# Mixer B's mask inside its scan, the sample's high and low parts in one set of 64 columns, even halves of 544 and 640 logits, norms spread by three copies, and gate loads let go earlier

## The chip, the core and the metric

The kernel runs on one core of a Trainium2 chip. Its engines are TensorE (PE, with its weight loads PEld), VectorE (DVE), ScalarE (ACT), GpSimd (POOL) and SyncE (SP), which issues nearly all DMAs. The metric is the device time of one execution in microseconds. Before the change it is 1721.83 us, the median of three runs (1721.07 to 1722.91).

## The reference

One layer of a streaming encoder is run for a prompt of 1024 tokens and for a sample of 32 new tokens behind a cache of 512. Weights are shared. Cut to what matters here:

```
z = rmsnorm(x) @ w_in            # q, k, v of mixer A; indexer q, k, w; q, k, v of mixer B; two gates

# mixer A: attention over the top-k keys that an indexer scores
score = (relu(q_i . k_i) * w_i).sum(heads);  idx = top_k(score)
o_a   = softmax(q . k[idx] / 8) @ v[idx]

# mixer B: stick-breaking attention, strictly causal
causal = kpos < qpos
sp   = where(causal, softplus(q . k / 8), 0)
tail = reverse_cumsum(sp) - sp
a    = where(causal, exp(log_sigmoid(q . k / 8) - tail), 0)
o_b  = a @ v

h = x + w_out(sigmoid(g_a) * (o_a @ w_ba) + sigmoid(g_b) * (o_b @ w_bb))
y = h + w_down(relu(w_up(rmsnorm(h)))**2)
```

Both mixers have eight heads of 64, the model's width is 1024 and the hidden width 4096. The keys, values and indexer keys are outputs as well.

## The kernel before, in words

**Precision.** Each fp32 operand is held as two parts of TensorE's round fp32 type, a high part (`xh`, `wh`) and the rest (`xl`, `wl`). A product is three matmuls: high by high, high by low, low by high. Casts on ACT make the high parts; subtractions on GpSimd or VectorE make the low ones.

**Stages.** The tokens are nine tiles of rows: eight of 128 for the prompt and one of 32 for the sample (`NEW`, tile 8). `run` (L535) goes through them so:

- the indexer's projections (`index_projection`, L789), with tokens stationary and weights moving, 328 or 256 columns. For the sample's tile, 32 token columns are stationary.
- `spread_rs` (L747): the reciprocal norms of the rows are needed along the free dimension as well. Each of nine tiles of 128 columns is made on GpSimd as `ones` times the norm, and transposed on TensorE.
- projections of mixer B (`project_b`), the indexer's scores (`index_scores`, L852) and a search for the top-k threshold on VectorE and ACT, which runs at low rank beside what follows.
- projections of mixer A (`project_a`, L1065): again tokens stationary, 256 columns, in four passes; `rope_tables` (L997) makes four tables of rotary factors before.
- mixer B: for each head `attend` (L1176) takes query tiles `t` of 128, with L = 128(t + 1) keys. The logits are made in pieces of 512 columns (PSUM banks `s`). `attend_new` (L1240) does the sample for four heads at once, over 512 cached and 32 new keys (`LS` = 544).
- mixer A: the same, in two passes over the heads, with softmax and the bfloat16 masks of the top-k.
- merge of the branches, the output projection, and the feed-forward part.

**Mixer B's weights** (`stick_weights`, L1146). ACT makes p = sigmoid(z) and rem = sigmoid(-z) from the logits. The reverse products of `rem` are a scan on VectorE, and GpSimd multiplies `p` with `rem` moved by one. The mask is added to the logits in PSUM before that, by one more matmul: `identr` stationary, and the triangle `trir` of -1e30 moving, 128 columns, on the tile's last piece (`tri4r`, 32 columns, for the sample). Then p is 0 and rem is 1 where a key isn't causal:

```
nc.vector.tensor_tensor_scan(rv, rv, rv, 1.0, op0=ALU.mult, op1=ALU.bypass)
nc.gpsimd.tensor_mul(p[:, 0:L - 1], p[:, 0:L - 1], rem[:, 1:L])
```

**What sets the order.** The program is not issued as it is written. Class `Plan` records every instruction as a node with its dependencies and a rank (FAST, PREP, MAIN, FILL, SLOW). It then issues each engine's nodes in order of a guessed time, by its own table of durations: the node that is ready first and, among the ready ones, the one of the lowest rank. Each engine then works through its list in that order. Work that can stand anywhere is used as filling for TensorE. `gate` (L1302) makes one of 16 blocks of 128 gate channels, whose matmuls write `pj` at rank FILL; ACT then takes a sigmoid, except for gates kept raw. Four are made before mixer B, four at its start, six beside its heads (`GATES_BESIDE`), and the last two, with 24 branch products, beside mixer A's heads (`FILL_BESIDE`). A DMA recorded inside `behind` or `held` is planned no earlier than a given node; `behind` takes the last node recorded, so a gate written after head h loads its weights no earlier than that head's end in the plan. Weights go through three buffers `wst`, ACT's cast into `wh` and a subtraction into `wl`, of which there are five pairs.

Every instruction goes through one line of `issue`, so nearly all rows of the profile carry L431; groups are told apart by the names of their tiles.

Of the kernel before, what the change touches and what calls it, by code (L numbers as in the profile page):

```python
# [13 lines left out]
I32 = mybir.dt.int32  # L14
AF = mybir.ActivationFunctionType
# [35 lines left out]
B11, B21, T1, T2, T3, T4, B22 = range(7)  # L51
FAST, PREP, MAIN, FILL, SLOW = 0, 1, 2, 3, 4


def rows(s):

    return DEC if s == NEW else 128

# [40 lines left out]
class Plan:  # L99
# [60 lines left out]
    def tile(self, pool, shape, dtype, name, tag=None, bufs=1, fine=False):  # L160
        tag = tag or name
        kw = {} if pool[2] is None and pool[3].startswith("d") else {"tag": tag, "bufs": bufs}
        t = pool[0].tile(shape, dtype, name=name, **kw)
        words = 1
        for s in shape[1:]:
            words *= s
        if dtype == BF16:
            words = (words + 1) // 2
        if kw:
            ring = self.rings.setdefault((pool[3], tag), [])  # L170
            old = ring[-bufs].touched if len(ring) >= bufs else ()
            psum = pool[3].startswith("ps") and not fine
            m = Mem(1 if psum else 4, 1 if psum else words, old, self.floors[pool[2]])
            ring.append(m)
        else:
            m = Mem(1, words * shape[0])
        self.mem[t.tensor.name] = m
        if pool[3].startswith("ps"):
            self.banks.add(t.tensor.name)
        if kw:  # L180
            self.onchip.add(t.tensor.name)
        self.members[pool[3]].append(m)
        return t


    def cells(self, ap):
        m = self.mem.get(ap.tensor.name)
        if m is None:
            return None
        if m.writer.shape == (1, 1):  # L190
            return m, slice(0, 1), slice(0, 1)
        size = 2 if ap.dtype == BF16 else 4
# [18 lines left out]
        return m, part, np.unique(idx) if size == 2 else idx  # L211
# [239 lines left out]
class Layer:  # L451
# [74 lines left out]

    def x_of(self, k, cs):
# [7 lines left out]
    def run(self):  # L535
# [24 lines left out]
        self.tri4r = nc.tile(self.wpool, [128, DEC], F32R, "tri4r")  # L560
# [8 lines left out]
        self.ones = c([128, 128], F32, "ones")  # L569
        nc.vector.memset(self.ones, 1.0)  # L570
        self.ident = c([128, 128], F32, "ident")
        self.identr = c([128, 128], F32R, "identr")
        self.trir = c([128, 128], F32R, "trir")
# [13 lines left out]
        for i, n in enumerate((W1, T - W1)):  # L587
            self.xh.append(nc.tile(xp, [128, KB, n], F32R, f"xh{i}"))
# [50 lines left out]
        self.att = self.pr = nc.open("att", "right")  # L639
        for _ in range(GATES_FIRST):  # L640
            self.gate(next(gates), "gz", 3)
        for h in range(H):
# [3 lines left out]
            with nc.behind():  # L646
# [22 lines left out]

        for h in range(H):  # L670
# [18 lines left out]
        self.ft = nc.tile(rp, [128, FWORDS], F32, "ft")  # L689
        self.turn = cycle(["pj", "a", "b", "c"])  # L690
# [11 lines left out]
    def constants(self):  # L702
        nc, a = self.nc, self.a
        for name, dst, n in (("tri", self.trir, 128), ("tri4", self.tri4r, DEC)):
            st = nc.tile(self.wpool, [128, 512], F32, name, tag="wst", bufs=3)
            nc.sync.dma_start(st[:, :n], a[name])
            nc.scalar.copy(dst, st[:, :n])
        nc.scalar.copy(self.identr, self.ident)
        nc.sync.dma_start(self.gf, a["g_ffn"])

    def normalise(self, sl):
# [4 lines left out]
        for hf in range(2):  # L716
# [7 lines left out]
            for kk in range(4):  # L724
# [22 lines left out]
    def spread_rs(self):  # L747

        nc = self.nc
        for sl in GROUPS:  # L750
            pt = self.bank("t")
            n = sum(rows(s) for s in sl)
            for i, s in enumerate(sl):
                b = nc.tile(self.ip, [128, 5 * HD], F32, "rsb", tag="ta", bufs=2)[:, :128]
                nc.gpsimd.tensor_scalar(b, self.ones, self.rs[:, s:s + 1], None, op0=ALU.mult)
                m = rows(s)
                nc.tensor.transpose(pt[:, i * 128:i * 128 + m], b[:m], self.ident[:m, :m])
# [3 lines left out]
    def index_setup(self):  # L761
# [9 lines left out]
        self.iw = [[None] * KB, None]  # L771

# [16 lines left out]
    def index_projection(self, part, s):  # L789
# [4 lines left out]
        if self.iw[part] is None:  # L794
# [7 lines left out]
            nc.scalar.copy(self.kih[:, T:], kc)  # L802
            nc.vector.tensor_sub(self.kil[:, T:], kc, self.kih.bitcast(F32)[:, T:])
# [4 lines left out]
        for k in range(KB):  # L808
            xh, xl = self.x_of(k, ts_)
            wh, wl = ws[k]  # L810
            nc.tensor.matmul(ps[:m, :n], xh, wh[:, :n], start=k == 0, stop=False)
            nc.tensor.matmul(ps[:m, :n], xh, wl[:, :n], start=False, stop=False)
            nc.tensor.matmul(ps[:m, :n], xl, wh[:, :n], start=False, stop=k == KB - 1)
# [21 lines left out]
        if part == 0:  # L835
# [6 lines left out]
            nc.scalar.copy(self.kih[:, ts_], pk[:, :m])  # L842
            nc.vector.tensor_sub(self.kil[:, ts_], pk[:, :m], self.kih.bitcast(F32)[:, ts_])

    def key_chunks(self, t):

        if t < 8:
            L = 128 * (t + 1)
            return [(c, min(512, L - c), c) for c in range(0, L, 512)]
        return [(0, PAST, T), (PAST, DEC, SEQ)]  # L850
# [99 lines left out]
    def top_k(self):  # L950

        nc, tp, tx, size = self.nc, self.top, self.top, self.size
        minus = nc.tile(tp, [128, 1], F32, "minus")
        nc.vector.memset(minus, -1.0)
        for g in self.groups:
# [19 lines left out]
            for j, t in enumerate(g.tiles):  # L975
# [13 lines left out]
                nc.scalar.activation(sq[:m, :L], pre[:m, :L], AF.Relu, bias=self.ones[:m, 0:1], scale=-1.0)  # L989
# [7 lines left out]
    def rope_tables(self):  # L997
# [9 lines left out]
        for j in range(2):  # L1007
            nc.vector.tensor_mul(self.tc_[:, :, j], C, g[:, j].unsqueeze(1).to_broadcast([128, NT, HD]))
            gx = g[:, j].rearrange("p (s e) -> p s e", s=2)[:, ::-1, :].unsqueeze(1).to_broadcast([128, NT, 2, 32])
            nc.vector.tensor_mul(  # L1010
# [54 lines left out]
    def project_a(self, p):  # L1065
# [7 lines left out]
        for s in range(NT):  # L1073
            m = rows(s)
            ts_ = slice(128 * s, 128 * s + m)
            ps = self.bank(PA_BANKS[s % len(PA_BANKS)])
            for k in range(KB):
                xh, xl = self.x_of(k, ts_)
                wh, wl = (u[:, (k % 2) * 256:(k % 2) * 256 + 256] for u in units[k // 2])
                nc.tensor.matmul(ps[:m, :256], xh, wh, start=k == 0, stop=False)  # L1080
                nc.tensor.matmul(ps[:m, :256], xh, wl, start=False, stop=False)
                nc.tensor.matmul(ps[:m, :256], xl, wh, start=False, stop=k == KB - 1)
# [63 lines left out]
    def stick_weights(self, parts, L, p, rem):  # L1146
# [6 lines left out]
        nc.vector.tensor_tensor_scan(rv, rv, rv, 1.0, op0=ALU.mult, op1=ALU.bypass)  # L1153
# [22 lines left out]
    def attend(self, h, is_a, passes=(0, 1)):  # L1176
# [17 lines left out]
        def weights(t, q, *room):  # L1194
# [3 lines left out]
            for c0 in range(0, L, 512):  # L1198
                n = min(512, L - c0)
                tail = not is_a and c0 + n == L  # L1200
                ps = self.bank("s")
                nc.tensor.matmul(ps[:, :n], qh, kk[:, c0:c0 + n], start=True, stop=False)
                nc.tensor.matmul(ps[:, :n], ql, kk[:, c0:c0 + n], start=False, stop=not tail)
                if tail:
                    nc.tensor.matmul(ps[:, n - 128:n], self.identr, self.trir, start=False, stop=True)
# [3 lines left out]
            return self.stick_weights(parts, L, *room)  # L1209

        for i in passes:
# [25 lines left out]
            with nc.rank(FAST):  # L1237
                nc.sync.dma_start(self.do[g, :, 512 * i:512 * i + 512], o)

    def attend_new(self, u, is_a):  # L1240
# [13 lines left out]
        kn = nc.tile(at, [128, 4, DEC], F32R, "kn", bufs=1)  # L1254
        nc.sync.dma_start(kn.bitcast(F32), self.dk[g0:g0 + 4, :, :, new].rearrange("j s e t -> (s e) j t"))
        for j in range(4):
# [3 lines left out]
            k = nc.tile(at, [128, SEQ], F32R, "kc", tag="k", bufs=3)[:, :PAST]  # L1260
            nc.scalar.copy(k[:HD], k32[:, j % 2])
            nc.gpsimd.tensor_sub(k[HD:], k32[:, j % 2], k.bitcast(F32)[:HD])
# [6 lines left out]
        parts = [(0, ps0[:, :]), (PAST, ps1[:, :DEC])]  # L1269
        if is_a:  # L1270
            p = self.softmax_weights(parts, LS, self.mask[8], self.fqs[:, u:u + 1], *self.rooms(is_a))
        else:
            nc.tensor.matmul(ps1[:, :DEC], self.identr, self.tri4r, start=False, stop=True)
            p = self.stick_weights(parts, LS, *self.rooms(is_a))
# [450 lines left out]
def _host_arrays(inp):  # L1725
# [45 lines left out]
    out["tri4"] = np.where(np.arange(DEC)[None, :] >= (i % DEC)[:, None], np.float32(NEG), np.float32(0)).astype(np.float32)  # L1771
    out["tri"] = np.where(i[None, :] >= i[:, None], np.float32(NEG), np.float32(0)).astype(np.float32)
# [36 lines left out]
```

## Time and profile before

| | |
|---|---|
| Median of three runs | 1721.83 us |
| The profiled execution, alone | 1724.92 us |
| Its span, first to last instruction | 1723.0 us |
| Mean granted TensorE clock | 0.997 |
| Chain that ended last, TensorE's share | 87% |
| Mixer B, first to last mask matmul | 484 to 686 us of the span |
| Table loads on ACT | 16, 20.5 us in all |
| DMA traffic | 289.08 MB, 168 GB/s |

A row of a group reads: line, engine, operation, tiles out<-in, shapes, count, then the busy time of the group, the mean duration of one in ns, and the idle time of the engine before them. A row of a timeline reads: start, duration, engine, line, operation, tiles, shapes, count of merged instructions. TensorE's matmuls overlap: a duration holds the way through the array, so the distance between starts says what one costs in a stream. A row of a table by stage gives, for each engine, busy time and instructions in that stretch, then the granted clock of TensorE, and the share and rate of the DMA engines.

### The profile page before, as it was taken

What the parts mean: (1) busy time and instruction counts of PE and PEld (TensorE: products, weight loads), DVE (VectorE), ACT (ScalarE), POOL (GpSimd) and SP (SyncE); (2) the same over time, 40 slices, a digit from 0 to 9 for tenths busy, and PEclk for the clock granted to TensorE, in tenths of its full rate; (3) what the DMA queues carried; (4) which work ended last, traced back from release to release, by engine and by line L of the source; (5) the groups of instructions that cost most, each with busy time, mean ns of one, the idle gap of its engine ahead of it and who ended that gap; (6) DMA issues with size and microseconds to landing.
All of it is one profiled execution on the core that took longest, in us unless ns stands there. A gap on an engine that the chain in (4) does not pass through costs nothing.

```text
span 1723.0 us, 34981 instructions
## 1 busy us (share of the span) xinstructions
PE 1691.1 (98%) x12356; PEld 1606.2 (93%) x12356; DVE 1346.7 (78%) x2773; ACT 952.8 (55%) x2023; POOL 854.2 (50%) x703
## 2 busy tenths in 40 slices
PE   7999999999999999999999999999999999999998
PEld 7988999899989899988999999999999999989998
DVE  8666899988568778775765648999988888797756
ACT  7455788765357768886655446333333444425431
POOL 5533331344367777365568757533333456556420
PEclk9999999999999999999999999999999999999999
DMA  7234453354673646686874643534443587756744
GB/s 255 82 100 126 128 161 116 89 151 139 172 207 101 172 103 173 177 243 190 243 213 148 179 135 116 165 135 152 136 153 132 189 286 245 266 169 232 255 127 149
DMA packets 182527, 289.08 MB, mean 168 GB/s; under 512 B 30800, under 2 KB 62128, under 8 KB 182352
## 3 DMA queue, kind: packets, MB, share of 16 engines
q1 hardware_dynamic: 182064, 286.50, 54.1%
q8 instruction: 98, 1.61, 0.4%
q14 instruction: 77, 0.63, 0.1%
q10 hardware_dynamic: 288, 0.34, 0.1%
HBM read 193.59 MB, written 93.07 MB: 166 GB/s over the span
## 4 chain that ended last, share of the span: by engine, by line
PE 87%; DVE 6%; DMA 3%; issue 1%; ACT 1%; POOL 1%; SPq 0%; DVEq 0%; ACTq 0%; POOLq 0%
PE pj L431 35%; PE s L431 11%; PE c L431 11%; PE b L431 10%; PE a L431 10%; PE t L431 5%; PE o L431 4%; DMA q<-dq 1%; DMA k<-cka 1%; DVE y L431 1%; DVE junk L431 1%; DVE us L431 1%; DVE mh L431 1%; DVE xl L431 1%; DMA xt<-x 0%
## 5 line engine op out<-in xcount | busy, mean ns | idle before, releaser
L431 POOL TENSOR_TENSOR wl<-wst,wh 128x512 fp32r<-128x512 f32 x160 | 229.5, 1440 | 231.0 <-ACT wh L431 172.3
L431 PE MATMUL pj<-xl,wh 128*128 128x272 f32 (+2 forms) x1200 | 336.4, 314 | 0.0
L431 PE MATMUL pj<-xh,wh 128*128 128x272 f32 (+1 forms) x768 | 253.3, 330 | 0.4 <-ACT sq L431 0.4
L431 PE MATMUL pj<-xh,wl 128*128 128x272 f32 (+1 forms) x768 | 252.6, 329 | 0.0
L431 PEld LDWEIGHTS pj<-xl,wh 128*128 128x128 f32 x1200 | 213.3, 189 | 11.4
L431 ACT CAST wh<-wst 128x512 fp32r<-128x512 f32 x213 | 131.1, 620 | 140.6 <-PE pj L431 23.4
L431 PEld LDWEIGHTS pj<-xh,wh 128*128 128x128 f32 x768 | 145.2, 189 | 11.5 <-ACT sq L431 0.7
L431 PEld LDWEIGHTS pj<-xh,wl 128*128 128x128 f32 x768 | 145.0, 189 | 10.5
L431 POOL TENSOR_TENSOR p<-p,rem 128x383 f32<-128x383 f32 (+8 forms) x66 | 110.7, 1697 | 31.8 <-DVE rem L431 25.1
L431 DVE TENSOR_TENSOR tt<-t,tt 128x512 fp32r<-128x512 f32 (+2 forms) x168 | 100.1, 620 | 33.2 <-ACT tt L431 32.7
L431 POOL TENSOR_TENSOR wl<-y,wh 128x512 fp32r<-128x512 f32 x49 | 72.9, 1490 | 96.1 <-ACT wh L431 93.0
L431 DVE TENSOR_TENSOR_SCAN rem<-rem 128x384 f32<-128x384 f32 (+8 forms) x66 | 110.6, 1696 | 9.7 <-ACT rem L431 9.6
L431 ACT CAST tt<-t 128x512 fp32r<-128x512 f32 (+2 forms) x168 | 85.8, 539 | 40.8 <-PE t L431 37.5
L431 ACT CAST wh<-y 128x512 fp32r<-128x512 f32 x79 | 49.1, 621 | 106.1 <-issue 23.0
L431 ACT CAST wh<-us 128x512 fp32r<-128x512 f32 x64 | 39.7, 622 | 114.6 <-PE pj L431 27.6
L431 PE MATMUL o<-tt,v 128*128 128x256 f32 (+1 forms) x640 | 99.0, 280 | 3.9 <-ACT tt L431 3.5
L431 ACT ACTIVATE junk<-score,cand 128x1024 bf16<-128x1024 f32 (+2 forms) x93 | 96.9, 1042 | 9.7 <-DVE cand L431 8.4
L431 PE MATMUL s<-k,q 128*128 128x512 f32 (+3 forms) x384 | 100.7, 357 | 1.3 <-DMA q<-dq 1.0
L431 PEld LDWEIGHTS o<-tt,v 128*128 128x128 f32 x640 | 91.8, 191 | 9.9 <-ACT tt L431 4.1
L431 DVE TENSOR_SCALAR_CACHE_REDUCE junk<-score,cand 128x384 bf16<-128x384 f32 (+1 forms) x124 | 92.9, 749 | 3.1
L431 PE MATMUL t<-ident,p 128*128 128x128 f32 (+1 forms) x596 | 91.0, 276 | 0.8 <-POOL p L431 0.6
L431 POOL TENSOR_TENSOR wl<-us,wh 128x512 fp32r<-128x512 f32 x33 | 50.3, 1533 | 71.3 <-ACT wh L431 71.3
(359 smaller groups left out, 5666.5 us busy)
## 6 DMA issues: line engine op xcount, KB each, us to landing
us<-w_down SPq DMA_DIRECT2D x80, 256.0 KB, 3.1
q<-dq SPq DMA_DIRECT2D x64, 256.0 KB, 4.9
du<-y SPq DMA_DIRECT2D x56, 264.0 KB, 2.5
du<-us SPq DMA_DIRECT2D x56, 264.0 KB, 2.5
y<-w_up SPq DMA_DIRECT2D x44, 256.0 KB, 2.7
k<-dk SPq DMA_DIRECT2D x40, 256.0 KB, 5.0
v<-dv SPq DMA_DIRECT2D x40, 256.0 KB, 4.4
xl<-du SPq DMA_DIRECT2D x35, 264.0 KB, 5.3
```

Source lines behind the costliest of these rows:

```text
L431: fn(*args, **kw)
```

## The change

1. Mixer B's mask leaves TensorE and moves into the scan: the state becomes max(state * rem, first), where `first` is a byte tensor that is 1 at the diagonal key and 0 elsewhere, and starts at 0. Keys that aren't causal give 0, the diagonal 1, and the products start there. One column of `p` is set to 0 by a memset, since its neighbour has no `rem`.
2. For the sample's tile, high and low parts stand side by side in `xh` as 64 stationary columns, so two matmuls for each block of the weights make four products (low by low too) in 64 rows, in place of three matmuls. `join` adds the lower 32 rows to the upper: an ACT copy and a VectorE add. The indexer's keys of the sample stand behind the cached ones.
3. Rows of 640 logits are made as 320 + 320 and those of 544 as 272 + 272 (`cut`). The sample's new keys get a DMA for each head into the tile of the cached ones.
4. `spread_rs` makes the broadcast norms of a group of tiles by one VectorE copy. The rotary tables' products move from VectorE to GpSimd.
5. A gate beside head h of mixer B is held to the end of that head's first pass rather than its second. The first piece of filling of mixer A is planned before its first head instead of after it.

```
+def cut(L):
+    return L // 2 if L in (640, LS) else 512
+MIDS = 1
+FILL_AHEAD = 1
-FILL_BESIDE = (1,1,1,1,2,2,2,2,2,2,2,2,2,2,2,1)
+FILL_BESIDE = (0,1,1,1,2,2,2,2,2,2,2,2,2,2,2,1)

+    def token_rows(self, ps, s, ws):
+        mm = self.nc.tensor.matmul
+        if s == NEW:
+            for k in range(KB):
+                x = self.xh[1][:, k, SEQ - W1:]
+                for i in range(2):
+                    mm(ps[:2 * DEC], x, ws[k][i], start=k + i == 0, stop=k + i == KB)
+            return
...
+    def join(self, ps, low):
+        self.nc.scalar.copy(low, ps[DEC:2 * DEC])
+        self.nc.vector.tensor_add(ps[:DEC], ps[:DEC], low)
...
+        if sl[-1] == NEW:
+            nc.scalar.copy(self.xh[1][:, :, T - W1:], self.xl[1].bitcast(F32)[:, :, SEQ - W1:])

         for _ in range(GATES_FIRST):
             self.gate(next(gates), "gz", 3)
+        self.mid = [None] * 3
         for h in range(H):
             self.attend(h, False)
             if h in (2, 5):
                 self.attend_new(h // 3, False)
-            with nc.behind():
+            with nc.held(self.mid[MIDS]):
                 for _ in range(GATES_BESIDE[h]):
                     self.gate(next(gates), "gz", 3)
...
+        beside(FILL_AHEAD)
         for h in range(H):
             self.attend(h, True, (0,))
             beside(FILL_BESIDE[h])
...
+            b = nc.tile(self.pr, [128, 2, 512], F32R, "rsb", tag="zz", bufs=2).bitcast(F32)[:, 0]
+            nc.vector.tensor_copy(b, self.rs[:, sl[0]:sl[-1] + 1].unsqueeze(2).to_broadcast([128, len(sl), 128]))
             for i, s in enumerate(sl):
-                nc.gpsimd.tensor_scalar(b, self.ones, self.rs[:, s:s + 1], None, op0=ALU.mult)
...
-            nc.vector.tensor_mul(self.tc_[:, :, j], C, g[:, j].unsqueeze(1).to_broadcast([128, NT, HD]))
+            nc.gpsimd.tensor_mul(self.tc_[:, :, j], C, g[:, j].unsqueeze(1).to_broadcast([128, NT, HD]))
...
-        nc.vector.tensor_tensor_scan(rv, rv, rv, 1.0, op0=ALU.mult, op1=ALU.bypass)
+        nc.vector.tensor_tensor_scan(rv, rv, one, 0.0, op0=ALU.mult, op1=ALU.max)
+        nc.vector.memset(p[:, L - 1:L], 0.0)
         nc.gpsimd.tensor_mul(p[:, 0:L - 1], p[:, 0:L - 1], rem[:, 1:L])
...
-            for c0 in range(0, L, 512):
+            for c0 in range(0, L, cut(L)):
-                if tail:
-                    nc.tensor.matmul(ps[:, n - 128:n], self.identr, self.trir, start=False, stop=True)
...
+            self.mid = self.mid[1:] + [len(nc.nodes) - 1]
...
-        nc.sync.dma_start(kn.bitcast(F32), self.dk[g0:g0 + 4, :, :, new].rearrange("j s e t -> (s e) j t"))
+            nc.sync.dma_start(k.bitcast(F32)[:, PAST:], self.dk[g0 + j, :, :, new].rearrange("s e t -> (s e) t"))
-                nc.tensor.matmul(ps0, q, k, start=first, stop=last)
-                nc.tensor.matmul(ps1[:, :DEC], q, kn[:, j], start=first, stop=is_a and last)
+                nc.tensor.matmul(ps0[:, :LS // 2], q, k[:, :LS // 2], start=first, stop=last)
+                nc.tensor.matmul(ps1[:, :LS // 2], q, k[:, LS // 2:], start=first, stop=last)
```

The plan is made anew, and with it the order on every engine up to the merge; from the merge on each engine's list is as it was. In number TensorE has 114 matmuls fewer, VectorE 73 instructions more, SP 11 DMAs more, and ACT loads its function tables 6 times in place of 16.

ACT, where mixer B ends and mixer A's first softmax begins (`gz` are the gates' sigmoids, `p,nb<-p,nb,fq` the softmax's exponentials, which use another table). Before:

```order
L431 ACTIVATE gz<-gz 128x512
L431 ACT_TABLE_LOAD
L431 ACTIVATE p,nb<-p,nb,fq 128x384
L431 COPY o<-o 64x256
L431 CAST tt<-t 128x512 x2
L431 ACTIVATE p,nb<-p,nb,fq 128x512
L431 ACT_TABLE_LOAD
L431 ACTIVATE gz<-gz 128x272
L431 ACT_TABLE_LOAD
L431 ACTIVATE p,nb<-p,nb,fq 128x128
```

And now:

```order
L440 ACTIVATE gz<-gz 128x272
L440 COPY o<-o 64x256
L440 CAST tt<-t 128x512 x2
L440 ACT_TABLE_LOAD
L440 ACTIVATE p,nb<-p,nb,fq 128x384
L440 COPY o<-o 64x256
L440 CAST tt<-t 128x512
L440 CAST tt<-t 128x384
L440 ACTIVATE p,nb<-p,nb,fq 128x512
```

The last gate sigmoids have moved ahead of the first exponential, so one table load stands there and no other follows until the merge.

SP, in the first pass of mixer A, where the sample's cached keys are loaded (`k_...<-cka`, two heads in each; `kn` and `kc<-dk` are the new keys; `wst<-w_bb` weights of the filling). Before:

```order
L431 DMA wst<-w_bb 128x512
L431 DMA gz<-dg 128x512
L431 DMA kn<-dk 128x4x32
L431 DMA k_7444<-cka 64x2x512
L431 DMA k_7447<-cka 64x2x512
L431 DMA dg<-gz 128x512
L431 DMA wst<-w_bb 128x512
```

And now:

```order
L440 DMA q<-dq 64x2x512
L440 DMA dg<-gz 128x512
L440 DMA k_7395<-cka 64x2x512
L440 DMA wst<-w_bb 128x512
L440 DMA k_7398<-cka 64x2x512
L440 DMA gz<-dg 128x512
L440 DMA dg<-gz 128x512
L440 DMA do<-o 64x512
L440 DMA wst<-w_bb 128x512
```

A load of weights has come between the two loads of cached keys, and new keys are no longer fetched at once beside them.

More of the change, by code (lines that the diff above doesn't have):

```diff
@@ L191, in cells @@
             return m, slice(0, 1), slice(0, 1)
-        size = 2 if ap.dtype == BF16 else 4
+        size = SMALL.get(ap.dtype, 4)
         dims = list(ap.ap)
@@ L210, in cells @@
         idx = idx * size // 4
-        return m, part, np.unique(idx) if size == 2 else idx
+        return m, part, np.unique(idx) if size < 4 else idx
     @staticmethod
@@ L559, in run @@
         self.gf = s([128, KB], "gf")
-        self.tri4r = nc.tile(self.wpool, [128, DEC], F32R, "tri4r")
+        self.eye4 = nc.tile(self.wpool, [128, DEC], F32, "eye4")
         w("wh3", "wl3")
@@ L639, in run @@
         self.att = self.pr = nc.open("att", "right")
+        self.first = nc.tile(self.att, [128, T], U8, "first")
+        nc.gpsimd.memset(self.first[:, DEC:SEQ + DEC - 128], 0)
+        nc.scalar.copy(self.first[:, :DEC], self.eye4)
+        nc.scalar.copy(self.first[:, SEQ + DEC - 128:], self.ident)
         for _ in range(GATES_FIRST):
             self.gate(next(gates), "gz", 3)
+        self.mid = [None] * 3
         for h in range(H):
@@ L689, in run @@
         self.ft = nc.tile(rp, [128, FWORDS], F32, "ft")
+        self.ones = nc.tile(rp, [128, 128], F32, "sum")
+        nc.vector.memset(self.ones, 1.0)
         self.turn = cycle(["pj", "a", "b", "c"])
@@ L703, in constants @@
         nc, a = self.nc, self.a
[L704 to L708, printed above, removed]
+        nc.sync.dma_start(self.eye4, a["eye4"])
         nc.sync.dma_start(self.gf, a["g_ffn"])
@@ L771, in index_setup @@
         self.iw = [[None] * KB, None]
+        self.ones = nc.tile(ik, [128, 128], F32, "ones")
+        nc.vector.memset(self.ones, 1.0)
     def index_weights(self, js):
@@ L807, in index_projection @@
         ps = self.bank("s")
[L808 to L813, printed above, removed]
+        self.token_rows(ps[:, :n], s, [[z[:, :n] for z in w] for w in ws])
+        if s == NEW:
+            self.join(ps[:, :n], nc.tile(self.wpool, [128, 512], F32, "pl", tag="wst", bufs=3)[:DEC, :n])
         w = nh * HD
@@ L952, in top_k @@
         nc, tp, tx, size = self.nc, self.top, self.top, self.size
-        minus = nc.tile(tp, [128, 1], F32, "minus")
+        minus, plus = (nc.tile(tp, [128, 1], F32, z) for z in ("minus", "plus"))
         nc.vector.memset(minus, -1.0)
+        nc.vector.memset(plus, 1.0)
         for g in self.groups:
@@ L1074, in project_a @@
             m = rows(s)
-            ts_ = slice(128 * s, 128 * s + m)
             ps = self.bank(PA_BANKS[s % len(PA_BANKS)])
[L1077 to L1082, printed above, removed]
+            self.token_rows(ps[:, :256], s, [
+                [u[:, i * 256:i * 256 + 256] for u in unit] for unit in units for i in range(2)])
+            if s == NEW:
+                self.join(ps[:, :256], nc.tile(pr, [128, 4, HD], F32, "pl", tag="sq", bufs=1).rearrange("p h e -> p (h e)")[:DEC])
             sq = nc.tile(pr, [128, 4, HD], F32, "sq", bufs=1)
@@ L1144, in softmax_weights, with stick_weights @@
         return p
-    def stick_weights(self, parts, L, p, rem):
+    def stick_weights(self, parts, L, p, rem, one):
         nc, at = self.nc, self.att
@@ L1208, in weights @@
                 return self.softmax_weights(parts, L, self.mask[t], self.fq[:, t, h:h + 1], room[0])
-            return self.stick_weights(parts, L, *room)
+            return self.stick_weights(parts, L, *room, self.first[:, DEC + SEQ - L:][:, ::-1])
         for i in passes:
@@ L1272, in attend_new @@
         else:
-            nc.tensor.matmul(ps1[:, :DEC], self.identr, self.tri4r, start=False, stop=True)
-            p = self.stick_weights(parts, LS, *self.rooms(is_a))
+            p = self.stick_weights(parts, LS, *self.rooms(is_a), self.first[:, :LS])
         pt = self.bank("t")
@@ L1770, in _host_arrays @@
     i = np.arange(128)
-    out["tri4"] = np.where(np.arange(DEC)[None, :] >= (i % DEC)[:, None], np.float32(NEG), np.float32(0)).astype(np.float32)
-    out["tri"] = np.where(i[None, :] >= i[:, None], np.float32(NEG), np.float32(0)).astype(np.float32)
+    out["eye4"] = (DEC - 1 - np.arange(DEC)[None, :] == (i % DEC)[:, None]).astype(np.float32)
     return out
```

56 lines of the change are left out of this document (29 added, 27 removed).

## The prediction

> **What bounds the kernel now.** I read the page's busy shares and the shares of its chain first.
>
> ```profile
> PE 1691.1 (98%) x12356; PEld 1606.2 (93%) x12356; DVE 1346.7 (78%) x2773; ACT 952.8 (55%) x2023; POOL 854.2 (50%) x703
> ...
> PE 87%; DVE 6%; DMA 3%; issue 1%; ACT 1%; POOL 1%; SPq 0%; DVEq 0%; ACTq 0%; POOLq 0%
> ```
>
> TensorE is busy for 98% of the span and carries 87% of the chain that ends last. No other engine comes near: VectorE, the next, has 78%. A matmul taken from TensorE's queue should therefore come off the end, wherever it stands, if nothing else takes its place. Busy time hides small gaps, so the second view is busy time by stage.
>
> ```profile
> core 0: us, PE busy (x) PEld busy (x) DVE busy (x) ACT busy (x) POOL busy (x), PEclk, DMA share, GB/s
> 0.00:90.00 90.00, 80.51 (x552) 74.75 (x553) 63.48 (x191) 51.80 (x134) 48.15 (x62) 1.00 0.50 161
> ...
> 300.00:340.00 40.00, 35.78 (x261) 33.17 (x260) 37.42 (x131) 30.32 (x62) 13.46 (x16) 0.96 0.29 91
> ...
> 485.00:694.00 209.00, 208.12 (x1447) 192.55 (x1447) 175.00 (x201) 154.47 (x364) 162.73 (x102) 1.00 0.54 147
> 694.00:740.00 46.00, 44.89 (x317) 41.46 (x317) 30.91 (x120) 42.81 (x83) 12.40 (x20) 1.00 0.68 190
> 740.00:897.00 157.00, 153.07 (x1048) 140.71 (x1046) 110.04 (x351) 108.36 (x227) 97.80 (x98) 0.99 0.78 223
> ...
> 950.00:1723.00 773.00, 761.31 (x6017) 749.82 (x6015) 626.02 (x996) 312.94 (x639) 367.48 (x265) 1.00 0.55 179
> ```
>
> The stages are the indexer's projections (0 to 90), part of mixer A's projections with the top-k counts (300 to 340), mixer B (485 to 694), the start of mixer A (694 to 740), the rest of it, and the merge with the feed-forward part. TensorE idles 9.5 us in the first (90 - 80.51), 4.2 in the second, 0.9 in mixer B, 1.1 and 3.9 in mixer A and 11.7 after 950. So 773 of the 1723 us hold no edit, and what is edited lies in stages where TensorE waits little.
>
> **The change part by part.** In a stream of matmuls the price of one is the distance from its start to the next start; its mean duration in the groups also holds the pipeline's depth. I take distances from timelines.
>
> *Masks.* 64 matmuls of 128 columns go (the tile `trir`), and two of 32 columns.
>
> ```profile
> 524.63 0.40 PE L431 MATMUL s<-k,q 128*128 128x256 f32 x2
> 524.87 0.22 PE L431 MATMUL s<-trir,identr 128*128 128x128 f32 x1
> 524.93 0.57 PE L431 MATMUL s<-k,q 128*128 128x384 f32 x2
> 525.34 0.28 PE L431 MATMUL o<-tt,v 128*128 128x256 f32 x1
> 525.46 0.22 PE L431 MATMUL s<-trir,identr 128*128 128x128 f32 x1
> 525.51 0.34 PE L431 MATMUL pj<-xh,wh 128*128 128x272 f32 x1
> 525.69 0.29 PE L431 MATMUL pj<-xl,wh 128*128 128x272 f32 x1
> ...
> 525.94 0.29 PE L431 MATMUL pj<-xh,wh 128*128 128x272 f32 x1
> ...
> L431 PE MATMUL s<-trir,identr 128*128 128x128 f32 x64 | 15.4, 240 | 0.0
> ```
>
> The mask at 525.46 is followed after 0.05 us, but the 272-column matmul behind it takes 0.18 instead of the 0.125 of each of the two after it (525.69 to 525.94): the short mask leaves no room to hide the next weight load. A mask thus costs 0.05 + 0.05 = 0.10 us, and by the pair at 524.87 0.06 + 0.06 (0.41 for two of 384 columns, against about 0.35 by the steps below). I take 0.11, so 66 x 0.11 = 7.3 us. Bounds are the bare distance, 66 x 0.05 = 3.3, and the group's whole 15.4.
>
> The Trainium skill, "TensorE: Matmul & The Clock Gate", section Back-to-back issue gap, gives N / 2.4 + 2.5 ns for a single matmul, about 56 ns at 128 columns; by that rule masks would be an estimated 3.7 us and the sum below 15.4. Its section on LDWEIGHTS gives columns / 1.2, which is 107 ns for 128 stationary columns, and the 0.10 to 0.12 measured above sides with it.
>
> *The sample's parts.* In each of six projections 24 matmuls of 32 stationary columns become 16 of 64.
>
> ```profile
> 313.06 0.28 PE L431 MATMUL s<-wh,xh 128*32 128x256 f32 x1
> 313.18 0.28 PE L431 MATMUL s<-wl,xh 128*32 128x256 f32 x1
> ...
> 315.86 0.29 PE L431 MATMUL pj<-xl,wh 128*128 128x272 f32 x1
> ...
> 51.01 0.31 PE L431 MATMUL s<-ih,xh 128*128 128x328 f32 x1
> 51.16 0.32 PE L431 MATMUL s<-il,xh 128*128 128x328 f32 x1
> ...
> L431 ACT COPY o<-o 64x256 f32<-64x256 f32 x68 | 25.1, 369 | 35.2 <-PE o L431 32.4 <-DMA do<-o 1.1 <-PE pj L431 0.6
> ```
>
> The 24 run from 313.06 to 315.86, 2.80 us or 0.117 each; a third less is 0.93, in five projections of 256 columns 4.7. The sixth has 328 columns at 0.15, so 8 x 0.15 = 1.2. Together 5.9 us. No row has 64 stationary columns, but 32 and 128 cost the same per moving column, so I put 64 there: the bounds are 5.9 and, if a matmul of 64 took half as long again, zero. Added is the join: an ACT copy and a VectorE add of 32x256, 0.37 us by the copy's row and about as much for the add, behind each projection. If TensorE had to wait for all six, that is 6 x 0.8 = 4.8 us; I cost it at nothing, because the next projection's `pj` matmuls stand in the queue. One copy of 8x32 columns into `xh` is added as well, once, of the same size.
>
> The skill's "TensorEngine Tiling (Array Packing)", section Key Properties, says that changing the tiling mode drains TensorE, which speaks against odd column counts: with a drain of 0.28 us (the flight time of the row at 313.06) on entering and leaving each of the six groups, an estimated 3.4 us, the sum below would be 15.6. No run here shows 64 columns, but the trace shows no such gap where the 32-column group ends.
>
> *Halves.* 512 + 128 columns become 320 + 320, and 512 + 32 become 272 + 272.
>
> ```profile
> 759.02 0.63 PE L431 MATMUL s<-k,q 128*128 128x512 f32 x2
> 759.49 0.40 PE L431 MATMUL pj<-xh,wh 128*128 128x512 f32 x1
> 759.72 0.34 PE L431 MATMUL s<-k,q 128*128 128x128 f32 x2
> 759.89 0.45 PE L431 MATMUL pj<-xl,wh 128*128 128x512 f32 x1
> 760.18 0.40 PE L431 MATMUL pj<-xh,wl 128*128 128x512 f32 x1
> ...
> 549.32 1.04 PE L431 MATMUL s<-kn,qz 128*128 128x32 f32 x8
> 550.21 0.26 PE L431 MATMUL s<-tri4r,identr 128*128 128x32 f32 x1
> ```
>
> A tile of 640 costs 0.47 for two of 512, 0.17 for two of 128 and 0.06 on the matmul behind them (0.29 instead of 0.23), 0.70 in all. 320 columns lie between 272 at 0.125 and 328 at 0.15, so four cost 4 x 0.147 = 0.59; 16 tiles save 16 x 0.11 = 1.8. For the sample the eight of 32 columns take 0.89 us, 0.11 each, as a full weight load would: a pair is 0.235 + 0.11 against 2 x 0.125, and 32 pairs save 3.1. In the indexer the same two cuts are made in eight heads each; the saving lies between nothing and 8 x 0.11 + 16 x 0.1 = 2.5, and I take 0.9. Halves together: 5.8 us, bounds 4.9 and 7.4.
>
> *VectorE, GpSimd, ACT.*
>
> ```profile
> L431 DVE TENSOR_TENSOR_SCAN rem<-rem 128x1024 f32<-128x1024 f32 x8 | 20.3, 2532 | 3.5 <-ACT rem L431 3.5
> L431 DVE TENSOR_TENSOR_SCAN pre<-sq,minus 128x1024 f32<-128x1024 bf16 x1 | 2.3, 2290 | 0.3 <-ACT sq L431 0.3
> ...
> 485.00:694.00 209.00, 110.58 (x66) 47.61 (x100) 109.92 (x66) 1.00 0.54 147
> ...
> L431 DVE MEMSET ss<- 128x9 f32 x1 | 0.1, 66 | 0.0
> L431 DVE TENSOR_TENSOR tabc<-ropec,gqk 128x576 f32<-128x576 f32 x2 | 1.5, 741 | 0.0
> ...
> L431 POOL TENSOR_TENSOR wl<-wst,wh 128x512 fp32r<-128x512 f32 x160 | 229.5, 1440 | 231.0 <-ACT wh L431 172.3
> ...
> L431 ACT ACT_TABLE_LOAD x11 | 14.1, 1283 | 0.2
> ```
>
> The scan gets a one-byte second operand and a maximum in place of a bypass. The one row with a narrower operand (bf16, 2290 ns) is not slower than the fp32 scans of that length (2532, some of them waiting), so I take no change. Bounds are the same time and, since nothing shows a byte operand, twice it (the last rival). The row of mixer B is that of instructions on `rem` alone, VectorE's first: scans hold it for 110.6 of 209 us. The 66 memsets of one column cost at most 66 x 0.066 = 4.4 us there, in the 34 us that VectorE idles (209 - 175.0). Spreading the norms takes nine products from GpSimd and gives VectorE three copies. The four rotary products (4 x 0.74 us) leave VectorE just before the stretch in which it is busy 37.42 of 40 us, and cost GpSimd about 4 x 1.6 (1440 ns for 512 columns, here 576), where it is busy 13.5 of 40; what they delay there is the low halves of weights, up to 6 us, and those are prepared ahead in five pairs of buffers. I cost both at nothing.
>
> The gates' loads are let go half a head earlier, and the first fill before mixer A's first head. By the order of instructions the last gate sigmoids then stand ahead of the first softmax, and ten of the table loads between 694 and 740 go: 10 x 1.28 = 12.8 us of ACT. ACT is busy 42.81 of those 46 us, but TensorE waits only 1.1, so this is worth 0 to 1.1 us. I count nothing.
>
> The sum is 7.3 + 5.9 + 5.8 = 19.0 us of TensorE. The profiled execution took 1724.92 us with its span of 1723.0, 3.1 over the median of 1721.83. It would come to 1705.9, and the median to 1702.8.
>
> **The rivals.** *Stalls shrink too.* ACT freed, VectorE relieved by 3 us around 300 to 340, fills earlier.
>
> ```profile
> PE t L431 <- DVE vt L431: 2.3, 1, 2.3
> ...
> 795.81 8.93 DMA k<-cka
> ```
>
> In the stretch 300 to 340 TensorE's longest wait, 2.3 us, is for VectorE, and its clock is at 0.96, which is another 0.04 x 40 = 1.6 us. In mixer A the cached keys take 8.93 us to land and ACT waits for them with the casts that TensorE needs behind it. All waits of 300 to 340 and 694 to 897 with the lost clock are 4.2 + 1.6 + 1.1 + 3.9 + 1.6 = 12.4; half of it gone gives 1697. Against it: the queue still issues those keys one weight load ahead of their cast.
>
> The skill's first page named above says in Part 1 that a few microseconds without work halve the clock for a window of about 3.4 us; the 0.96 behind that wait agrees.
>
> *New stalls take part of it.* The scheduler laid out the first 940 us anew, and its idea of times missed by 2 to 4 us at two places. Against 19.6 us of waits there now (9.5 + 4.2 + 0.9 + 1.1 + 3.9), half as many again makes 1713; twice as many would leave the time where it was.
>
> *The work goes, but not from the path*, so that the time stays within 0.2%, about what a measurement of this kernel can tell from none: it needs TensorE waiting about 16 us more, against 98% busy.
>
> *Slower: the scan.* If a one-byte operand or the maximum makes the scan slower, VectorE becomes mixer B's bound. It has 34 us of room less 4 for memsets, so this decides from a scan 27% slower (30 of 110.6), costs back the 19 from 45%, and at twice the time adds 110.6 - 30 = 81, so 1784. The bf16 row speaks against it.
>
> **How the numbers follow.** The forecast (1699 to 1708) has 0.55, shrinking stalls 0.17, new stalls 0.18, no change 0.05 and the slow scan or anything slower 0.05. The predicted time is 1703. The bounds of the costs (masks 3.3 to 15.4, joins up to 4.8) widen it to 1694 to 1713, which leaves out the last two cases and the ends of the others. Faster has 0.9, within 0.2% 0.05, slower 0.05.
>
> **What would show it.** TensorE's count must fall by 114. In mixer B a scan of 1024 should stay at 2.3 to 2.6 us and VectorE under 185. The 64-column matmuls should follow each other at 0.117 us, those of 320 at 0.147. Table loads should be 6, not 16. The rows from 950 on should keep their length; if TensorE's idle time before 950 is over 28 us, the new order made stalls, and if it is under 14, it took some away. The prediction is wrong if the span falls by less than 10 us or more than 28.

## The result, and the profile after

| | before | changed |
|---|---|---|
| median, us | 1721.8 (1721.07 to 1722.91) | 1705.38 (1703.88 to 1707.35) |
| ratio | | 0.9901, 95% interval 0.9889 to 0.9914 |
| profiled execution, us (span) | 1724.92 (1723.0) | 1703.88 (1702.1) |

The change gains 16.4 us by the medians; 1703.0 was forecast, and the forecast's own range of 1699 to 1708 holds the time. The two profiled executions differ by 21.0: that of before lies 3.1 over its median, that of the changed kernel 1.5 under. So 4.6 us of what two traces show is spread between executions.

The page of the changed kernel, busy shares and chain:

```profile
PE 1671.8 (98%) x12242; PEld 1591.3 (93%) x12242; DVE 1349.7 (79%) x2846; ACT 942.4 (55%) x2019; POOL 847.7 (50%) x699
...
PE 85%; DVE 8%; issue 2%; DMA 2%; ACT 1%; POOL 1%; SPq 0%; DVEq 0%; ACTq 0%; POOLq 0%
```

TensorE has the 114 matmuls less that were counted, and 19.3 us less busy time. Its idle time, the span less that, is 30.3 us where it was 31.9 (1723.0 - 1691.1). The same comes from distances between matmul starts. As the time of a matmul I take (columns + 29) / 2.4 ns, a fit to the distances measured (0.125 us at 272 columns, 0.146 at 320), but no less than 0.11 us, the distance at which those of 128 or 32 columns follow each other. What the distances exceed this by, where it is over 60 ns, adds up to 65.9 us of waits before and 63.1 now, stretches at half clock included; the rest of the stream is 17.8 us shorter. The split rests on that fit: without the 0.11 the rest would be 14.5 us shorter.

Busy time by stage of the changed kernel, with bounds where its stages lie now (busy us of each engine, TensorE's clock, DMA share, GB/s):

```profile
0.00:84.00 84.00, 75.39 (x515) 71.01 (x516) 65.95 (x187) 52.33 (x132) 42.08 (x52) 1.00 0.54 172
...
300.00:340.00 40.00, 38.07 (x290) 35.74 (x289) 38.75 (x137) 30.81 (x64) 15.07 (x18) 1.00 0.37 105
...
474.00:690.00 216.00, 214.04 (x1481) 198.47 (x1481) 179.50 (x269) 156.05 (x368) 157.61 (x102) 1.00 0.53 145
690.00:736.00 46.00, 41.73 (x284) 36.49 (x283) 39.42 (x167) 40.97 (x107) 21.43 (x36) 1.00 0.84 230
736.00:882.00 146.00, 144.82 (x1015) 134.50 (x1014) 100.73 (x307) 98.45 (x193) 91.05 (x86) 1.00 0.78 231
...
913.00:1702.00 789.00, 777.53 (x6144) 766.10 (x6143) 641.00 (x1012) 320.21 (x655) 382.08 (x276) 1.00 0.54 178
```

The last stage, 789 us with 11.5 of idle, is what it was. In the 40 us of top-k counts TensorE idles 1.9 us where it idled 4.2, and its clock is back at 1.00. After the start of mixer A it idles 1.2 where it idled 3.9. At that start itself the reverse has come: 4.3 us of 46, against 1.1. Between the same events of the two programs, 3.9 us go up to the top-k counts, 6.8 from there to mixer B's first scan, and 10.2 in the two mixers.

What the prediction named, by group (count, busy us, mean ns of one | idle of the engine before them):

```profile
L440 DVE TENSOR_TENSOR_SCAN rem<-rem,first 128x1024 f32<-128x1024 f32 x8 | 21.9, 2742 | 3.0 <-ACT rem L440 1.8 <-POOL p L440 1.1
L440 DVE MEMSET p<- 128x1 f32 x66 | 3.8, 59 | 6.0 <-ACT p L440 3.3 <-DMA dg<-gz 2.4
L440 POOL TENSOR_TENSOR tabs<-ropes,gqk 128x576 f32<-128x576 f32 x2 | 2.9, 1438 | 0.0
L440 ACT ACT_TABLE_LOAD x6 | 7.7, 1283 | 3.8 <-DMA gz<-dg 2.0 <-PEq L1819 1.7
```

And the sample's columns of one projection, where they begin on TensorE's timeline (start, us, stationary rows * columns):

```profile
312.08 0.28 PE L440 MATMUL s<-wh,xl 128*128 128x256 f32 x1
312.20 0.28 PE L440 MATMUL s<-wh,xh 128*64 128x256 f32 x1
312.31 0.28 PE L440 MATMUL s<-wl,xh 128*64 128x256 f32 x1
```

The scan's mean is above the 2532 of before, and above the 2.3 to 2.6 us that the prediction set as its mark. But the eight differ much among themselves, from 2287 to 3521 ns now and from 2292 to 2984 then, and the shortest are alike. All 66 scans take 113.9 us, where they took 110.6. VectorE is busy 179.5 of mixer B's 216 us. The 64-column matmuls follow each other at 0.11 to 0.12 us.

### The profile page after: what moved, and what is told of

It is laid out like the page before. It is cut to its first block, busy times and chain, and to the rows that moved or that the text cites. A ratio compares the mean times of both kernels' runs of the same rounds, so it can differ in the third digit from the quotient of the medians.

```text
span 1702.1 us, 34820 instructions
## 1 busy us (share of the span) xinstructions
PE 1671.8 (98%) x12242; PEld 1591.3 (93%) x12242; DVE 1349.7 (79%) x2846; ACT 942.4 (55%) x2019; POOL 847.7 (50%) x699
## 4 chain that ended last, share of the span: by engine, by line
PE 85%; DVE 8%; issue 2%; DMA 2%; ACT 1%; POOL 1%; SPq 0%; DVEq 0%; ACTq 0%; POOLq 0%
PE pj L440 35%; PE c L440 11%; PE b L440 10%; PE a L440 10%; PE s L440 10%; PE o L440 5%; PE t L440 5%; DVE junk L440 2%; DVE y L440 1%; DVE mh L440 1%; DVE us L440 1%; POOL wl L440 0%; SPq L440 0%; DVE wl L440 0%; DVE small L440 0%
## 5 line engine op out<-in xcount | busy, mean ns | idle before, releaser
L440 PEld LDWEIGHTS pj<-xh,wh 128*128 128x128 f32 x768 | 144.6, 188 | 10.2 <-DVE gz L440 0.3
L440 POOL TENSOR_TENSOR p<-p,rem 128x383 f32<-128x383 f32 (+8 forms) x66 | 101.8, 1562 | 45.3 <-DVE rem L440 34.3
L440 DVE TENSOR_TENSOR_SCAN rem<-rem,first 128x384 f32<-128x384 f32 (+8 forms) x66 | 113.9, 1748 | 7.5 <-ACT rem L440 6.3
L440 ACT ACTIVATE junk<-score,cand 128x1024 bf16<-128x1024 f32 (+2 forms) x93 | 97.0, 1043 | 12.3 <-DVE cand L440 10.7
L440 PE MATMUL s<-k,q 128*128 128x512 f32 (+4 forms) x384 | 97.9, 353 | 5.6 <-DVE nb L440 3.0
```

What stands on the lines that cost most here:

```text
L440: fn(*args, **kw)
```

## The experiments

The gain of each is against runs of before on the same chip. Busy is TensorE's on the page of the profiled execution, idle the span less that.

| kernel | median, us | gain | ratio (95%) | busy | idle |
|---|---|---|---|---|---|
| changed | 1705.38 | 16.4 | 0.9901 (0.9889 to 0.9914) | 1671.8 | 30.3 |
| changed, again | 1705.89 | 15.5 | 0.9911 (0.9895 to 0.9926) | 1668.7 | 32.5 |
| masks back on TensorE | 1709.99 | 12.4 | 0.9926 (0.9914 to 0.9939) | 1678.0 | 30.5 |
| masks of zeros added | 1712.79 | 9.6 | 0.9942 (0.9930 to 0.9955) | 1677.8 | 33.3 |
| sample in 32 columns | 1709.91 | 12.4 | 0.9922 (0.9907 to 0.9937) | 1673.3 | 28.8 |
| halves cut at 512 | 1710.91 | 11.4 | 0.9930 (0.9918 to 0.9943) | 1676.1 | 30.4 |
| gates as before | 1711.17 | 10.3 | 0.9936 (0.9923 to 0.9949) | 1675.9 | 35.1 |
| norms, rotary as before | 1713.18 | 8.2 | 0.9947 (0.9936 to 0.9959) | 1673.8 | 39.2 |
| before, mask alone | 1722.35 | -0.9 | 1.0004 (0.9996 to 1.0013) | 1685.9 | 34.7 |
| before, mask, order kept | 1717.32 | 4.2 | 0.9975 (0.9963 to 0.9986) | 1686.6 | 30.8 |
| before, side edits alone | 1715.26 | 6.2 | 0.9969 (0.9958 to 0.9981) | 1687.9 | 28.7 |
| changed, side edits undone | 1718.16 | 3.3 | 0.9978 (0.9969 to 0.9988) | 1676.1 | 40.6 |
| changed, filling let go earlier | 1701.99 | 21.0 | 0.9873 (0.9853 to 0.9893) | 1670.9 | 31.6 |

### Each cut in TensorE's stream undone

Masks back:

```
-        nc.vector.tensor_tensor_scan(rv, rv, one, 0.0, op0=ALU.mult, op1=ALU.max)
-        nc.vector.memset(p[:, L - 1:L], 0.0)
+        nc.vector.tensor_tensor_scan(rv, rv, rv, 1.0, op0=ALU.mult, op1=ALU.bypass)
...
+                if tail:
+                    nc.tensor.matmul(ps[:, n - 128:n], self.identr, self.trir, start=False, stop=True)
```

> The changed kernel with mixer B's mask back on TensorE (66 matmuls) and the old scan without the memset of one column. If the masks cost what the prediction says, 0.11 us each in the stream, the time is 1705.4 + 7.3 = 1712.7 us. If only their own distance to the next start counts (5.2 us by the trace of before), 1710.6. If the new scan and its memsets took something of it back on VectorE, less than 1710. If the order made anew matters more than the matmuls, anything within 4 us of 1712.7, with TensorE's waits before 950 us differing from the changed kernel's by that much.

Masks of zeros, which leave the scan of the change in place:

```
+                if tail:
+                    nc.tensor.matmul(ps[:, n - 128:n], kk[:, :128], self.zero.unsqueeze(1).to_broadcast([128, 16, 8]), start=False, stop=True)
```

> The changed kernel, scan and all, with 66 matmuls put where the masks were, which add zeros to the logits (for stationary columns the keys, for moving ones a tile of zeros): the masks' price on TensorE by itself. Theory: 1705.4 + 7.3 = 1712.7 us, as for the kernel with the masks back; own distance alone: 1710.6. If the scan of the change costs VectorE something that the end sees, this kernel is slower than the one with the masks and the old scan, by that.

The sample in 32 columns (`join` and the copy into `xh` go too):

```
-                for i in range(2):
-                    mm(ps[:2 * DEC], x, ws[k][i], start=k + i == 0, stop=k + i == KB)
...
+            xh, xl = self.x_of(k, slice(128 * s, 128 * s + rows(s)))
```

> The changed kernel with the sample's projections as before: 24 matmuls of 32 stationary columns in place of 16 of 64, no join. The product of the two low parts is left out, as before. Theory: 48 matmuls at 0.117 to 0.15 us, 1705.4 + 5.9 = 1711.3 us. Rival, that the joins cost TensorE up to 0.8 us each: 1705.4 + 5.9 - 4.8 = 1706.5.

Halves:

```
-    return L // 2 if L in (640, LS) else 512
+    return 512
...
-                nc.tensor.matmul(ps0[:, :LS // 2], q, k[:, :LS // 2], start=first, stop=last)
+                nc.tensor.matmul(ps0[:, :PAST], q, k[:, :PAST], start=first, stop=last)
```

> The changed kernel with rows of 640 logits as 512 + 128 and of 544 as 512 + 32 again. Theory: 1705.4 + 5.8 = 1711.2 us, of which 3.1 from the sample's logits, 1.8 from the attention's 640 and 0.9 from the indexer. Rival: the short matmuls lay in gaps that are there anyway, 1705 to 1707.

With the changed kernel at 1705.6 (the mean of its two medians) they cost 4.4, 7.2, 4.3 and 5.3 us, each uncertain by some 3 (its own interval and the changed kernel's together). In the traces, waits set aside, the stream grows by 7.4, 6.6, 5.1 and 5.4. The prices of the prediction (7.3, 7.3, 5.9, 5.8) are right to within a microsecond, in the stream. The times by themselves don't settle a mask's price: the kernel with the masks back (1710.0) came out near the bare distance (1710.6), that with masks of zeros (1712.8) at the theory (1712.7). Of the masks undone the end saw 3.0 us less than the stream, no more than the uncertainty. Whether the new scan costs anything at the end isn't settled either: the two kernels with masks differ by 2.8 us, and their intervals overlap. On VectorE the 66 scans take 113.8 us with the masks back, where the scan is the old one, and 110.0 with masks of zeros, where it is the new one.

### The side edits undone

The changed kernel was timed again, with two others beside it on the same chip. The gates as before:

```
-FILL_AHEAD = 1
+FILL_AHEAD = 0
...
-            with nc.held(self.mid[MIDS]):
+            with nc.behind():
```

And the norms and rotary tables as before:

```
-            nc.vector.tensor_copy(b, self.rs[:, sl[0]:sl[-1] + 1].unsqueeze(2).to_broadcast([128, len(sl), 128]))
+                nc.gpsimd.tensor_scalar(b, self.ones, self.rs[:, s:s + 1], None, op0=ALU.mult)
...
-            nc.gpsimd.tensor_mul(self.tc_[:, :, j], C, g[:, j].unsqueeze(1).to_broadcast([128, NT, HD]))
+            nc.vector.tensor_mul(self.tc_[:, :, j], C, g[:, j].unsqueeze(1).to_broadcast([128, NT, HD]))
```

> The changed kernel as it is, on the chip of the three that follow. All theories: 1705.4 us within 2; the others of this call are compared with it.

> The changed kernel with the gates of mixer B and the first filling of mixer A held as before. In the changed kernel TensorE idles 4.6 us between 690 and 740 us, where it idled 1.1 between 694 and 740. Theory of the prediction (the edit is worth nothing): 1705.4. Rival A, that the looser gates took work out of the start of mixer A and made these waits: they go, about 1702, TensorE idle in that stretch 1 to 2 us, and ACT's table loads there come back to ten or so. Rival B, that they removed more waits than they made, by freeing ACT of table loads (TensorE's idle from 740 to 885 is 0.8 us, from 740 to 897 before 3.9): 1708 or more.

> The changed kernel with the nine products that spread the norms back on GpSimd and the rotary tables' four products back on VectorE. Theory of the prediction: no difference, 1705.4. Rival: VectorE is full around 300 to 340 us, and its 3 us of products there bring back the wait for vt that is gone in the changed kernel, with the half clock behind it: TensorE idle from 300 to 340 at 4 in place of 1.9, clock 0.96, 1708 to 1709.

Both edits that the prediction costed at nothing count: 5.3 and 7.3 us against the changed kernel on the same chip, each uncertain by some 3. Where they work is seen in the list of TensorE's waits (engine, line, waited for: us in total, times, longest). Without the norms and rotary edit, from 300 to 480 us:

```profile
PE pj L440 <- DVE tb L440: 2.5, 2, 2.0
PE t L440 <- DVE vt L440: 2.0, 1, 2.0
PE t L440 <- DVE vs L440: 1.5, 1, 1.5
PE pj L440 <- DVE vt L440: 0.9, 1, 0.9
```

And in the changed kernel there:

```profile
PE t L440 <- DVE az L440: 1.1, 1, 1.1
PE s L440 <- ACT wh L440: 0.6, 1, 0.6
```

Five waits for VectorE, 6.9 us, stand against three of 1.6, of which the longest is shown. From the first product `qk` of mixer A's projections to mixer B's first scan it takes 181.3 us in place of 174.3. These 7.0 us are as much as the medians lost; the two traces differ by 10.9, and most of the rest lies in the mixers.

Without the gates' edit the wait of before at the cached keys is back. The view of the loads `k<-cka` says who waited for them, in all and how often: in the kernel before, the changed one, and the one with the gates as before:

```profile
  ACT kc L431: 5.4, 3
```

```profile
  ACT kc L440: 0.9, 2
```

```profile
  ACT kc L440: 4.2, 2
```

TensorE waits 2.3 us behind it in that profile, and later in mixer A it idles once more and loses clock:

```profile
800.00:885.00 85.00, 83.06 (x561) 77.49 (x561) 57.83 (x180) 53.46 (x105) 48.56 (x47) 0.96 0.77 225
```

```profile
870.30 0.41 ACT L440 CAST vcs<-vc 128x256 fp32r<-128x256 f32 x1 [1.78 <-DMA vc<-cva]
870.78 0.73 POOL L440 TENSOR_TENSOR vcs<-vc,vcs 128x256 fp32r<-128x256 f32 x1 [2.29 <-ACT vcs L440]
871.72 0.70 PE L440 MATMUL s<-k,q 128*128 128x512 f32 x2 [1.94 <-issue]
```

Idle 1.9 us and a clock of 0.96, worth 3.4 us there, stand beside the 2.3: together more than the 5.3 us lost, in one profile that is 8.9 longer than the changed kernel's. The idle time ends 0.2 us after GpSimd has made the low part of the cached values (`vcs`), for whose load ACT had waited 1.8 us. The profile names no releaser, so that late values cause it is likely, not shown. Rival A is out: its waits at the start of mixer A stay (4.9 us of idle from 692 to 738). Rival B holds as to the time, but not for the reason it gave. The table loads that came back are two, 2.6 us of ACT, not ten; what is seen before TensorE's wait of 2.3 us is the late load of the keys, not ACT's tables.

### One half of the change alone

The mask alone in the kernel before, by the lines of the change (the tile `first` with them):

```
-        nc.vector.tensor_tensor_scan(rv, rv, rv, 1.0, op0=ALU.mult, op1=ALU.bypass)
+        nc.vector.tensor_tensor_scan(rv, rv, one, 0.0, op0=ALU.mult, op1=ALU.max)
+        nc.vector.memset(p[:, L - 1:L], 0.0)
...
-                if tail:
-                    nc.tensor.matmul(ps[:, n - 128:n], self.identr, self.trir, start=False, stop=True)
```

> The kernel before with nothing but the mask moved into the scan: 66 matmuls less, the byte operand, the memsets. Theory: 1721.8 - 7.3 = 1714.5 us. Rival, that VectorE's 66 memsets and the new scan take a part of it back (the kernel with zero masks stood 2.8 above that with masks and the old scan): 1717.

Nothing is gained, though 66 matmuls are gone. The planner makes a new order for the shorter stream, and some 840 of TensorE's 12,300 rows have moved in it, beside the 66 that are gone. So I kept the order: the planner counts a matmul that is not issued, and counts nothing for the memsets. In the trace TensorE's rows then stand exactly as before, with the masks left out.

```
+    def ghost(self, eng, op, *args, **kw):
+        self.record(eng, lambda *a, **k: None, op, args, kw)
...
+                    nc.ghost(PE, "matmul", ps[:, n - 128:n], kk[:, :128], kk[:, :128])
...
+        with nc.free_of_cost():
+            nc.vector.memset(p[:, L - 1:L], 0.0)
```

> The kernel before with the mask in the scan, as in the kernel with the mask alone, but the planner still counts the 66 masks and counts nothing for the memsets, so that every engine keeps the order of before, with the masks gone from TensorE's and the memsets put into VectorE's. Theory C, that the masks' 7 us were lost to a new order when the mask alone was changed: here they are gained, 1721.6 - 7 = 1714.6 us. Theory D, that the kernel waits for VectorE or transfers there anyway, whatever the order: within 2 us of 1721.6, TensorE's stream 7 us shorter and its waits 7 us longer.

It gains 4.2 us, between both theories. About five microseconds (4.2 + 0.9, uncertain by some 2.5) lie in the order alone. Of the 6.9 us by which its stream is shorter, mixer B's waits take back some: from 484 to 686 us they are 12.3 us by distances of starts, where they were 9.7.

Then the side edits alone, put into the kernel before:

```
-            with nc.behind():
+            with nc.held(self.mid[MIDS]):
...
+        beside(FILL_AHEAD)
...
+            nc.vector.tensor_copy(b, self.rs[:, sl[0]:sl[-1] + 1].unsqueeze(2).to_broadcast([128, len(sl), 128]))
...
-            nc.vector.tensor_mul(self.tc_[:, :, j], C, g[:, j].unsqueeze(1).to_broadcast([128, NT, HD]))
+            nc.gpsimd.tensor_mul(self.tc_[:, :, j], C, g[:, j].unsqueeze(1).to_broadcast([128, NT, HD]))
```

> The kernel before with nothing but the norms spread in three copies, the rotary products on GpSimd, and the looser gates: no matmul less. Undone in the changed kernel these were worth 7.3 and 5.3 us. If they remove waits that are there whatever TensorE does, 1721.6 - 12.6 = 1709 us. If they only make room for the shorter stream of matmuls, 1719 to 1722. The wait for vt between 300 and 340 us should be gone in both cases, with the half clock behind it: at least 3 us less there.

And the cuts in the stream alone, which is the changed kernel with both undoings of the section above:

```
-            with nc.held(self.mid[MIDS]):
+            with nc.behind():
...
-            nc.gpsimd.tensor_mul(self.tc_[:, :, j], C, g[:, j].unsqueeze(1).to_broadcast([128, NT, HD]))
+            nc.vector.tensor_mul(self.tc_[:, :, j], C, g[:, j].unsqueeze(1).to_broadcast([128, NT, HD]))
```

> The changed kernel with both side edits undone (norms, rotary products, gates): only the matmuls of masks, sample and halves are changed, the 19.0 us of the prediction. If the prices simply add, 1721.6 - 17.8 (TensorE's stream shorter, by the traces) = 1704. If the side edits are worth in the changed kernel what their undoing cost, 1705.9 + 12.6 = 1718.

The side edits alone gain 6.2, the cuts alone 3.3, and both together 16: more than their sum by 6.5. By distances of starts, the side edits alone leave the stream as long as it was and lower the waits from 65.9 to 59.8 us, and the cuts alone raise them to 77.3; with both they are 63.1. The 14.2 us by which the side edits lower them beside the cuts lie for 5.4 in mixer A's projections and for 5.1 in mixer A, the stages that those edits touch. In the kernel with the cuts alone the page shows TensorE at 1676.1 busy, 15.0 less than before, and idle for 40.6 us, 8.7 more. One of the new waits, first on VectorE's timeline:

```profile
398.66 2.19 DVE L440 TENSOR_TENSOR_SCAN pre<-sq,minus 128x768 f32<-128x768 bf16 x1
...
401.32 1.62 DVE L440 SCALAR_TENSOR_TENSOR pre<-pre,needb,sgn 128x768 f32<-128x768 f32 x1
402.86 0.41 DVE L440 TENSOR_TENSOR ta<-pj,tabc 128x256 f32<-128x256 f32 x1
403.19 0.41 DVE L440 TENSOR_TENSOR tb<-pj,tabs 128x256 f32<-128x256 f32 x1
```

And TensorE's:

```profile
401.28 0.28 PE L440 MATMUL s<-wl,xh 128*64 128x256 f32 x1
401.40 0.38 PE L440 MATMUL t<-ident,qk 128*128 128x128 f32 x2
403.75 0.47 PE L440 MATMUL pj<-xh,wh 128*128 128x512 f32 x1 [1.97 <-DVE tb L440]
```

The sample's 16 matmuls end at 401.4, a microsecond sooner than 24 would. The next projection needs the bank that VectorE empties with `ta` and `tb`, and these stand behind the top-k's scan and its next step, 3.8 us. So a microsecond saved here only lengthens the wait. In the whole change VectorE has 3 us less to do ahead of this stretch, and the wait is gone.

That is one wait of 2 us, and it shows one way in which the two halves make room for each other. It doesn't show the whole 6.5 us, since both kernels also have a new order: some 1,080 of TensorE's rows have moved with the side edits alone, against before, and 1,160 with the cuts alone, against the changed kernel. No run takes these halves apart with the order kept, so what is room and what is order stays open.

### The wait that the change made

In the changed kernel's mixer A the largest wait of TensorE is for VectorE's part of the softmax, and the first filling's weights come late to ACT, by the list of waits and by its timeline:

```profile
PE s L440 <- DVE nb L440: 3.0, 2, 1.6
```

```profile
713.11 0.62 ACT L440 CAST wh<-wst 128x512 fp32r<-128x512 f32 x1 [0.78 <-DMA wst<-w_g]
```

The last run lets go that filling two passes earlier, and moves one piece of filling from mixer A's second pass to its first head:

```
-FILL_BESIDE = (0,1,1,1,2,2,2,2,2,2,2,2,2,2,2,1)
+FILL_BESIDE = (1,1,1,1,2,2,2,2,2,1,2,2,2,2,2,1)
...
-        beside(FILL_AHEAD)
+        beside(FILL_AHEAD, self.mid[0])
```

> The changed kernel with the first filling of mixer A let go two passes earlier (at the end of mixer B's last head but one), one more piece beside mixer A's first head and one less beside its second pass. Theory, that TensorE waits at the start of mixer A because the first filling's weights come late: the waits of the first 46 us of mixer A (8.8 us in the profile of the changed kernel) fall to 4 or less, and the time from 1705.6 to about 1701. Rival, that VectorE's and ACT's chain of the first softmax sets that stretch: the waits stay at 8 to 9, the time at 1705.

It is the fastest of all, 1702.0 us, by its time as the theory said; its interval still touches that of the changed kernel. Its profile doesn't bear the theory out: the waits of those 46 us are 6.8 us, where 4 or less was said and the changed kernel has 8.8, and in mixer A new ones for `q` have come (2.4 us). That profiled execution was the slowest of its four (1704.37), so where the rest was gained isn't shown.

## Why the prediction was right, point by point

- **What the matmuls cost** held. The stream is 17.8 us shorter where 19.0 was summed: masks 6.6 to 7.4 (7.3), the sample's columns 5.1 to 5.9 (5.9; by the distances of its own matmuls 17.9 us before and 12.0 now), halves 5.4 (5.8). The rule of the Trainium skill, "TensorE: Matmul & The Clock Gate", section Back-to-back issue gap, by which masks would be an estimated 3.7 us, is given there for an isolated matmul; in this stream masks cost more. The drain of the Trainium skill's "TensorEngine Tiling (Array Packing)", section Key Properties, comes with a change of the tiling mode, and nothing like it is seen with narrower weights: at 312 us the next start after the step from 128 columns to 64 comes in 0.12 us, as from 64 to 64.
- **"A matmul taken from TensorE's queue should therefore come off the end, wherever it stands"** failed. With the cuts alone 3.3 us of some 17.6 came off, with the mask alone none. That TensorE is 98% busy didn't save the step: it waits behind VectorE and loads in short stretches, what it does faster there it waits longer, and the new order takes its part.
- **"I cost both at nothing" and "I count nothing"** for norms, rotary products and gates failed. They were worth 6.2 us alone and 7.3 and 5.3 beside the cuts. The prediction had the row for it, VectorE busy 37.42 of 40 us, and put it among the rivals (*stalls shrink too*, half of 12.4 us).
- So the sum came out within 2.6 us by luck, because two errors cancelled: 19.0 us were counted for cuts that alone yield 3.3, and nothing for side edits that beside them yield some 13.
- *New stalls take part of it* is seen at the start of mixer A, 4.3 us of idle for 1.1, and bought back elsewhere. The slow scan is out by the shortest scans, 2287 against 2292 ns, and the 66 together are 3% longer, not 27 (113.9 against 110.6 us). None of TensorE's waits is put down to a join.
- Of the marks it named, these came: 114 matmuls, table loads 6, VectorE under 185 in mixer B, starts of 64-column matmuls 0.117 us apart and of those of 320 columns 0.146, the rows from 950 on unchanged, TensorE's idle before them 18.8 us, between 14 and 28. One was missed: the mean scan of 1024 takes 2.74 us, not 2.3 to 2.6.

## What to carry to other kernels

A busy share of 98% says which engine to relieve, not that each microsecond taken from it is gained: ask for each stretch which engine releases the next matmul, and whether that one gets free sooner. Edits that seem worth nothing, because they free an engine off the path, can decide what a cut on the path yields; test a cut alone and the rest alone before summing prices. Where a planner makes the order, an edit also changes the order, and that was worth about 5 us here; keeping the order with counted but unissued work tells the two apart.

## What the runs showed of the hardware

Executions of one kernel spread as much as one edit is worth: the changed kernel's ten lie between 1703.0 and 1712.6 us. A scan of 1024 with a byte as second operand and a maximum takes as long as one in fp32 with a bypass (shortest 2287 and 2292 ns). Stationary widths of 32, 64 and 128 cost the same per moving column (starts 0.117 to 0.118 us apart at 256 columns).
